# The two operands of the opening's norm move from the tag of the decay floors' logits into two tiles of their own

## The chip, the cores and the metric

The kernel runs on one core of a Trainium2 chip. The metric is the device time of one execution in microseconds (us); a program's time is the median of its runs. The core's engines each run their own list of instructions strictly in order: PE (matmul; PEld is its weight load), DVE (vector), ACT (scalar and activation), POOL, and SP, which here only issues transfers. An instruction that waits holds up everything behind it on its engine; an issue of a transfer that waits holds up all later issues of SP.

## The reference, cut to what matters

The kernel computes two layers of a decoder trunk on 512 tokens of width 1024. Only the very beginning is touched: the first normalisation and the first feed-forward block.

```python
def rms_norm(x, gain):
    inv = lax.rsqrt(jnp.mean(x * x, axis=-1, keepdims=True) + EPS)
    return (x * inv) * gain

def swiglu(h, w_in, w_out):                       # w_in 1024 x 5632, w_out 2816 x 1024
    gate, up = jnp.split(h @ w_in, 2, axis=-1)
    return (jax.nn.silu(gate) * up) @ w_out

x = x + 0.5 * swiglu(rms_norm(x, ffn1_norm[0]), ffn1_w_in[0], ffn1_w_out[0])   # the opening is in here
...                                               # three token mixers; a second swiglu; the same for layer 1
```

One of the mixers, HGRN2, has a decay with a floor per channel: `lower_bounds`, a softmax over the layers of `hgrn_lb_logits` (2 x 256 numbers, 2 KB), is computed once, in the opening, and first used much later.

## The kernel before, in words

**Products.** x is held transposed, as eight tiles of 128 features by 512 tokens. Every float32 product is made of three matmuls: each operand is parted into a high part (rounded to the format fp32r by a copy on ACT) and a low part (operand minus high part, a subtraction on DVE), and PE adds high*high, high*low and low*high. In `mm3` these are lines 318, 324 and 325; in the opening's own loop all three are line 1710.

**Weights.** A *granule* is two steps k of 128 rows of the weights by 512 columns, 512 KB. `granule` (line 282) loads it by two transfers of 256 KB issued by SP (line 290) into a staging tile `st` (two buffers), and `parted` writes its high part (line 307, ACT) and its low part (line 308, DVE) into an `hl` tile (three buffers). An `st` buffer is free again when line 308 has read it, an `hl` buffer when PE has used it. The casts of such granules are given high priority, so the scheduler sets them as early in each engine's list as it believes their data to be there.

**The opening** (`open_stream`, line 1631). Blocks f = 0, 2, 4 of the first feed-forward (two tiles of gate and two of up columns each, four PSUM banks, 96 matmuls of 512 columns) are multiplied plainly, by `cover` (line 491); from f = 6 on an arrangement with fewer products (`halved`) takes over, with matmuls of 256 columns. During f = 0, x itself arrives: SP loads x and the weights in turn, PE transposes x (line 1647), ACT and DVE make the scaled high and low parts of x (lines 391, 392) and of the weights (lines 1666, 1667), DVE copies x (line 1732), and ACT squares it (line 407) for DVE to add up in `sqacc` (line 408). The order of these loads on SP, and of most of the rest, is given by hand (`follow`); what is not given, the scheduler orders by priority and by its own estimate of the times. These three blocks use the raw x times gain, so their products don't need the norm; the norm's factor `inv` is multiplied in when their banks are cleared (lines 548, 549).

**The norm of the opening** (`norm` in `cover`, line 503). `parted_norm` (line 418) parts `sqacc` into two tiles of 128 x 512, high by ACT, low by DVE (both line 421). `end_norm` (line 427) sums both over the features with two matmuls (line 430) into one PSUM bank, here `po`, of which there is one buffer, and makes `inv` from it: three ACT instructions (line 270), then DVE lines 414, 415 and 416. Then `halves_of_x` (line 691) makes the operands of the halved blocks from x and `inv` (lines 701 to 740).

**The logits.** Right after `norm()`, `cover` calls `lower_bounds` with one scratch tile (line 523). Its transfer (line 956) is put into SP's given order, ahead of the loads of f = 2. Its arithmetic is 20 small DVE instructions (lines 958 to 997) and two small ACT ones.

**Tags.** A tile pool gives each tag a number of buffers; a tile asked for under a tag takes one of them, and its first writer waits until the last reader of that buffer's former tile is done. Tag `g1` has two buffers. Before the change the norm's high and low part are the first two tiles of `g1`, and the scratch tile of the logits is the third. Tags `r0` and `r1`, with one buffer of 4 KB per partition each, hold quarters of the hidden activations; their first writers are lines 686 and 689, behind the clearing of f = 0.

```python
def norm():
    self.end_norm(self.bank(...), fp, self.parted_norm(fp, "g1", 2))                              # 504
    ...
self.lower_bounds(logits, fp.tile([P, T], F32, tag="g1", name=self.n("lb"), bufs=2))            # 523
self.follow("s", nc.sync.dma_start(lg, logits.rearrange("l (r p) -> p l r", p=P)))              # 956
```

Of the kernel before, what the change touches and what calls it, by code (L numbers as in the profile page):

```python
# [9 lines left out]
F32R = mybir.dt.float32r  # L10
# [13 lines left out]
P = 128  # L24
T = 512
# [131 lines left out]
class Trunk:  # L157
# [257 lines left out]
        V(nc.vector.tensor_scalar(t, t, scalar1=-0.5, scalar2=1.5, op0=ALU.mult, op1=ALU.add))  # L415
        V(nc.vector.tensor_mul(out, r, t))

    def parted_norm(self, pool, tag, bufs, keep=False):
        nc = self.nc
        hi, lo = (pool.tile([P, T], F32R, tag=tag, name=self.n("sh"), bufs=bufs) for _ in range(2))  # L420
        a, b = nc.scalar.copy(hi, self.sqacc), nc.vector.tensor_sub(lo, self.sqacc, hi)
        if keep:
            self.follow("a", a)
            self.follow("v", b)
        return hi, lo
# [65 lines left out]
    def cover(self, fp, w_in, covered, begin, then):  # L491
        nc = self.nc
        x, gain, logits = begin
        for f in range(0, covered, 2):
            banks = self.next4()

            def parts(k, kk, f=f):
                r = slice(k * P, (k + kk) * P)
                return [w_in[r, f * P : (f + 2) * P], w_in[r, FF + f * P : FF + (f + 2) * P]]

            opening = f == 0

            def norm():
                self.end_norm(
                    self.bank("pt" if self.ntog % 2 == 0 else "po"), fp,
                    self.parted_norm(fp, "g1", 2),
                )
                self.xparts = self.halves_of_x(fp)

                for _ in range(2):  # L510
                    next(self.xparts)


            jobs = [(bk, slice(c, c + P)) for bk, c in zip(banks, (0, 256, 128, 384))]
            if opening:
                self.open_stream(x, gain, fp, parts, jobs)
            else:
                self.stream([(*j, None) for j in jobs], parts, self.xact, KD, queued=f == 2)
            if opening:
                nt = iter(["xh4", "xl4", "xh5", "xl5", "xh6", "xl6", "r2", "r3", "r4", "r5"])  # L520
                self.build_consts(lambda dt: fp.tile([P, T], dt, tag=next(nt), name=self.n("c")))
                norm()
                self.lower_bounds(logits, fp.tile([P, T], F32, tag="g1", name=self.n("lb"), bufs=2))
            if f == 2:
                for _ in self.xparts:
                    pass
            if f + 4 == covered or f + 2 == covered:
                next(then)
            if opening:
                self.table(SILU)  # L530

            def finish(i, f=f, banks=banks):
                self.finish(fp, f, i, banks[2 * i], banks[2 * i + 1], f + 2 == covered)

            if f + 2 < covered:
                for i in range(2):
                    finish(i)
        return finish
# [20 lines left out]
    def enter(self, fp, w_in, then):  # L559
        nc = self.nc  # L560
        H = T // 2
        A, V = (lambda i, e=e: self.follow(e, i) for e in "av")

        def stream(f, banks, given):
            def parts(k, kk):
                r = slice(k * P, (k + kk) * P)
                return [w_in[r, f * P : (f + 2) * P], w_in[r, FF + f * P : FF + (f + 2) * P]]

            return self.stream_steps(
                [(bk, slice(c, c + P), None) for bk, c in zip(banks, (0, 256, 128, 384))],  # L570
                parts, self.xact, KD, given=given,
            )

        ba = self.next4()
        first = stream(0, ba, lambda k: k == KD - 2)
        for _ in range(4):
            next(first)
        parts = self.parted_norm(fp, "g1", 2, True)
        nb = self.bank("pt" if self.ntog % 2 == 0 else "po")
        bb = self.next4()  # L580
        second = stream(2, bb, lambda k: True)
        self.ngain = self.const.tile([P, KD], F32, tag="ngain", name=self.n("ngain"))
        A(nc.scalar.activation(self.ngain, self.gain, AF.Copy, scale=-1.0))
        next(second)
        self.end_norm(nb, fp, parts, True)
        self.table(SILU)
        next(first, None)
        next(then)
        X, self.xc, lows = {}, {}, {}

        def quarter(a, b):
            X[a, b] = t = fp.tile([P, 4, H], F32, tag=f"r{2 + 2 * a + b}", name=self.n("xn"))
            for k in range(4):
                i = 4 * a + k
                V(nc.vector.scalar_tensor_tensor(
                    out=t[:, k, :], in0=self.xT[:, i, b * H : (b + 1) * H],
                    scalar=(self.gain if a == b else self.ngain)[:, i : i + 1],
                    in1=self.inv[:, b * H : (b + 1) * H], op0=ALU.mult, op1=ALU.mult,
                ))

        def high(name):
            c = ORDER_IN.index(name)
            src, other = X[SUM[name]], name in NEGATIVE
            hi, lo = (
                fp.tile([P, 4, H], F32R, tag=f"x{w}{c}", name=self.n("xc")) for w in "hl"
            )
            self.xc[name] = hi, lo
            A(nc.scalar.activation(hi, src, AF.Copy, scale=-1.0) if other else nc.scalar.copy(hi, src))

            def low():  # L610
                V(nc.vector.scalar_tensor_tensor(
                    out=lo, in0=src, scalar=-1.0, in1=hi, op0=ALU.mult, op1=ALU.subtract
                ) if other else nc.vector.tensor_sub(lo, src, hi))

            lows[name] = low

        def add(x, y):
            V(nc.vector.tensor_add(X[x], X[x], X[y]))

        def both(name):  # L620
            high(name)
            lows[name]()

        def row():
            next(second)
            next(second, None)

        cleared = {}

        def clear(f, i):  # L630
            banks = bb if f else ba
            cleared[f, i] = self.clear(fp, banks[2 * i], banks[2 * i + 1], True)

        def values(f, i):
            self.values(fp, f, i, *cleared.pop((f, i)), True)

        quarter(0, 0)
        high("P1")
        quarter(1, 0)
        lows["P1"]()  # L640
        next(second)
        next(second)
        high("P2")
        quarter(0, 1)
        lows["P2"]()
        quarter(1, 1)
        next(second)
        next(second)
        add((0, 0), (0, 1))
        high("P5")  # L650
        clear(0, 0)
        lows["P5"]()
        next(second)
        next(second)
        next(second, None)
        add((0, 0), (1, 1))
        high("P6")
        self.given["total"]()
        lows["P6"]()
        self.given["prepare"](0)  # L660
        self.given["prepare"](1)
        clear(0, 1)
        add((0, 1), (1, 1))
        next(then)
        values(0, 0)
        self.entry = {
            0: lambda: both("P7"),
            1: lambda: (both("P3"), add((0, 0), (1, 0))),
            3: lambda: both("P4"),
            7: lambda: values(0, 1),  # L670
            9: lambda: clear(2, 0),
            10: lambda: values(2, 0),
            12: lambda: clear(2, 1),
            13: lambda: values(2, 1),
        }
# [323 lines left out]
    def mix(self, l, w, w_out, conv_w, out_gain, q_gain, k_gain, f_bias, next_gain):  # L999
# [3 lines left out]
        with tc.tile_pool(name=self.n("mix"), bufs=1) as mp:  # L1003
# [47 lines left out]
            with tc.tile_pool(name=self.n("hg"), bufs=1) as hp:  # L1051
                self.tt, self.tb = "t", 3
                norm = lambda: self.end_norm(
                    self.bank("pt"), hp, self.parted_norm(hp, self.tt, self.tb)
                )
                bz = features([(H_F, 256)], ("mm", "mm"), norm)
                bg = features([(H_G, 256)], ("mm", "po"))
# [728 lines left out]
```

## Time and profile before

| | |
|---|---|
| median of 3 runs | 1832.18 us (1830.63 to 1835.08) |
| profiled execution | 1827.76 us, its span from first to last instruction 1826.0 us |
| mean granted PE clock | 0.998 |
| PE busy | 1809.0 us, 99% of the span |
| DVE busy | 1466.3 us, 80% |
| ACT busy | 989.9 us, 54% |

The profile shows one execution. In the timeline view each row gives start, duration (us), engine, line, operation and tiles, and in brackets the idle time of that engine before it and what ended it. Rows named SPq are issues of transfers. The waits view sums such idle time: total, times, longest. The windows view gives each engine's busy time in a stretch; its column PEclk is the granted clock of PE (1.00 is full speed).

### The profile page before, as it was taken

The page shows a single profiled execution, that of the slowest core. Times are in us where ns is not written, and L with a number is a line of the kernel's source. Part 1 is how long each engine was busy: PE and PEld are TensorE (multiplying, and loading weights), DVE is VectorE, ACT ScalarE, POOL GpSimd, SP SyncE. Part 2 cuts the span into 40 slices and gives each one's busy share as a digit, 9 for nine tenths or more (in the row PEclk, how much of TensorE's full clock was granted, in tenths as well). Part 3 has the DMA queues.
Part 4 walks back from the last instruction along what each step waited for, and adds up shares of the span by engine and source line. Part 5 has one row for each costly group of instructions (what it writes and reads, how often), then busy time and mean ns, then how long its engine had stood idle before and what let it go on. Part 6 is the DMA issues. An engine that isn't in the chain of part 4 may idle for free.

```text
span 1826.0 us, 34831 instructions
## 1 busy us (share of the span) xinstructions
PE 1809.0 (99%) x14345; PEld 1684.3 (92%) x14345; DVE 1466.3 (80%) x2017; ACT 989.9 (54%) x1402; POOL 169.5 (9%) x168
## 2 busy tenths in 40 slices
PE   8999999999999999999999999999999999999999
PEld 6899999899878899999889999998997788999997
DVE  8788888676797988879678887866858878888883
ACT  5455555454675565555445555555547665555551
POOL 0011020100000001112001111201000000020210
PEclk9999999999999999999999999999999999999999
DMA  5849684233322767868265787813333228677762
GB/s 147 233 109 199 171 174 113 70 88 83 87 71 92 216 141 163 191 168 174 81 193 137 162 191 194 165 64 82 83 82 82 76 93 231 162 152 195 153 137 92
DMA packets 243935, 250.94 MB, mean 137 GB/s; under 512 B 18457, under 2 KB 229153, under 8 KB 243777
## 3 DMA queue, kind: packets, MB, share of 16 engines
q1 hardware_dynamic: 189872, 182.38, 32.8%
q0 software_dynamic: 53600, 66.09, 22.7%
q8 instruction: 112, 1.84, 0.4%
q14 instruction: 47, 0.38, 0.1%
q10 hardware_dynamic: 304, 0.27, 0.0%
HBM read 223.98 MB, written 2.10 MB: 124 GB/s over the span
## 4 chain that ended last, share of the span: by engine, by line
PE 92%; DVE 3%; ACT 3%; DMA 1%; issue 1%; SPq 0%; ACTq 0%; DVEq 0%
PE mm L318 13%; PE mm L325 13%; PE mm L324 13%; PE sc L325 6%; PE sc L324 6%; PE sc L318 6%; PE pt L318 6%; PE pt L324 6%; PE pt L325 6%; PE po L318 3%; PE po L324 3%; PE po L325 3%; PE po L1543 1%; PE sc L1710 1%; PE pt L1710 1%
## 5 line engine op out<-in xcount | busy, mean ns | idle before, releaser
L786 ACT CAST hl<-w 128x1024 fp32r<-128x1024 f32 x322 | 337.5, 1051 | 317.9 <-PE mm L325 76.8
L788 DVE TENSOR_TENSOR hl<-w,hl 128x1024 fp32r<-128x1024 f32 x322 | 392.7, 1222 | 85.8 <-ACT hl L786 85.6
L307 ACT CAST hl<-st 128x512 fp32r<-128x512 f32 (+2 forms) x188 | 142.2, 756 | 190.3 <-PE po L325 67.8
L308 DVE TENSOR_TENSOR hl<-st,hl 128x512 fp32r<-128x512 f32 (+2 forms) x188 | 161.6, 860 | 100.3 <-ACT hl L307 98.6
L318 PE MATMUL mm<-xc,hl 128*128 128x256 f32 (+1 forms) x732 | 201.7, 276 | 0.5 <-ACT g L897 0.5
L325 PE MATMUL mm<-xc,hl 128*128 128x256 f32 x728 | 201.6, 277 | 0.0
L324 PE MATMUL mm<-xc,hl 128*128 128x256 f32 x728 | 201.5, 277 | 0.0
L325 PE MATMUL sc<-xc,hl 128*128 128x256 f32 x528 | 146.0, 277 | 0.0
L318 PE MATMUL sc<-xc,hl 128*128 128x256 f32 (+1 forms) x530 | 146.0, 276 | 0.0
L324 PE MATMUL sc<-xc,hl 128*128 128x256 f32 x528 | 145.9, 276 | 0.0
L318 PEld LDWEIGHTS mm<-xc,hl 128*128 128x128 f32 x732 | 137.3, 188 | 0.8 <-ACT g L897 0.7
L324 PEld LDWEIGHTS mm<-xc,hl 128*128 128x128 f32 x728 | 137.0, 188 | 0.0
L325 PEld LDWEIGHTS mm<-xc,hl 128*128 128x128 f32 x728 | 136.7, 188 | 0.1
L318 PE MATMUL pt<-xc,hl 128*128 128x256 f32 (+1 forms) x484 | 132.9, 276 | 0.0
L324 PE MATMUL pt<-xc,hl 128*128 128x256 f32 x480 | 132.7, 277 | 0.0
L325 PE MATMUL pt<-xc,hl 128*128 128x256 f32 x480 | 132.5, 276 | 0.0
L318 PE MATMUL mm<-x,hl 128*128 128x512 f32 x272 | 108.5, 399 | 6.0 <-ACT hl L307 5.6
L324 PE MATMUL mm<-x,hl 128*128 128x512 f32 x272 | 107.5, 395 | 0.0
L325 PE MATMUL mm<-x,hl 128*128 128x512 f32 x272 | 107.1, 394 | 0.0
L318 PEld LDWEIGHTS sc<-xc,hl 128*128 128x128 f32 x530 | 99.5, 188 | 0.2
L325 PEld LDWEIGHTS sc<-xc,hl 128*128 128x128 f32 x528 | 99.1, 188 | 0.1
L324 PEld LDWEIGHTS sc<-xc,hl 128*128 128x128 f32 x528 | 99.1, 188 | 0.0
(510 smaller groups left out, 5618.2 us busy)
## 6 DMA issues: line engine op xcount, KB each, us to landing
w<-in_ffn_w_in_dram SPq DMA_DIRECT2D x140, 512.0 KB, 5.2
w<-in_ffn_w_out_dram SPq DMA_DIRECT2D x64, 512.0 KB, 4.5
w<-in_ffn_w_out_dram POOLq DMA_DIRECT2D x56, 512.0 KB, 8.6
st<-in_w_mix_in_dram SPq DMA_DIRECT2D x88, 256.0 KB, 2.7
st<-in_ffn_w_in_dram SPq DMA_DIRECT2D x70, 256.0 KB, 3.3
w<-in_ffn_w_in_dram POOLq DMA_DIRECT2D x35, 512.0 KB, 8.5
w<-S POOLq DMA_DIRECT2D x35, 512.0 KB, 4.8
st<-in_ffn_w_out_dram SPq DMA_DIRECT2D x24, 512.0 KB, 4.6
```

The costliest lines, as they stand in the source:

```text
L307: a = nc.scalar.copy(hi, src[:, c : c + w])
L308: b = nc.vector.tensor_sub(lo, src[:, c : c + w], hi)
L318: i = nc.tensor.matmul(acc[:, c], ah, bh[:, c], start=first and c.start == 0, stop=False, skip_group_check=True,)
L324: nc.tensor.matmul(acc, ah, bl, start=False, stop=False, skip_group_check=True)
L325: i = nc.tensor.matmul(acc, al, bh, start=False, stop=last, skip_group_check=True)
L786: A(nc.scalar.copy(hi, src))
L788: return lambda: V(nc.vector.tensor_sub(lo, src, hi))
L1543: nc.tensor.matmul(self.ob[:, t0 + u * P : t0 + 2 * P], V[:, j, h % 4].rearrange("p a d -> p (a d)"), part[:, j, u:, :].rearrange("p i t - ...
L1710: E(nc.tensor.matmul(acc, wh[j][l][:, cols], (self.xh, self.xl)[r][k + j], start=k + j == 0 and which == 0, stop=k + j == KD - 1 and which ...
```

## The change

`parted_norm` takes one tag for each of its two tiles. In the opening these become `r0` and `r1`; the two other callers pass the tags that they had. The logits' scratch tile keeps `g1` and is now its first tile.

```diff
-    def parted_norm(self, pool, tag, bufs, keep=False):
+    def parted_norm(self, pool, tags, bufs, keep=False):
         nc = self.nc
-        hi, lo = (pool.tile([P, T], F32R, tag=tag, name=self.n("sh"), bufs=bufs) for _ in range(2))
+        hi, lo = (pool.tile([P, T], F32R, tag=tag, name=self.n("sh"), bufs=bufs) for tag in tags)
@@ cover
-                    self.parted_norm(fp, "g1", 2),
+                    self.parted_norm(fp, ("r0", "r1"), 1),
@@ enter
-        parts = self.parted_norm(fp, "g1", 2, True)
+        parts = self.parted_norm(fp, ("g1", "g1"), 2, True)
@@ mix
-                    self.bank("pt"), hp, self.parted_norm(hp, self.tt, self.tb)
+                    self.bank("pt"), hp, self.parted_norm(hp, (self.tt,) * 2, self.tb)
```

The number of instructions and of bytes moved stays the same. The scheduler's lists differ in the opening only.

## The prediction

> **What bounds the kernel now.** I read the shares on the page first, then what PE waited for, what SP's issues waited for, then the opening row by row in the timeline.
>
> ```profile
> PE 1809.0 (99%) x14345; PEld 1684.3 (92%) x14345; DVE 1466.3 (80%) x2017; ACT 989.9 (54%) x1402; POOL 169.5 (9%) x168
> ```
>
> PE bounds the whole; only time in which PE stands still or runs slowly can be won. The largest of PE's waits in the first 150 us, then the one among those of SP's issues that bears on it (total, times, longest):
>
> ```profile
> PE mm L318 <- ACT hl L307: 5.6, 1, 5.6
> ```
>
> ```profile
> SPq L956 <- DVE sh L421: 15.7, 1, 15.7
> ```
>
> PE's largest wait is for the first weights of block f = 2. SP could not load them, because the 2 KB of logits ahead of them stood 15.7 us for a `g1` buffer until the norm's low part (L421) had been made, and a little longer until PE had used it. The rows:
>
> ```profile
> 19.99 0.67 DVE L1667 TENSOR_TENSOR hl<-st,hl 128x512 fp32r<-128x512 f32 x1
> ...
> 24.50 0.69 ACT L391 ACTIVATE x<-po,gain 128x512 fp32r<-128x512 f32 x1
> 25.08 0.62 ACT L1666 CAST hl<-st 128x512 fp32r<-128x512 f32 x1
> ...
> 26.02 0.75 DVE L392 SCALAR_TENSOR_TENSOR x<-po,gain,x 128x512 fp32r<-128x512 f32 x1
> 26.38 2.93 PE L1710 MATMUL sc<-x,hl 128*128 128x512 f32 x12
> 26.68 0.68 DVE L1667 TENSOR_TENSOR hl<-st,hl 128x512 fp32r<-128x512 f32 x1
> 27.28 0.69 DVE L1732 COPY xT<-mm 128x512 f32<-128x512 f32 x1
> ...
> 29.14 2.89 PE L1710 MATMUL pt<-x,hl 128*128 128x512 f32 x12
> ...
> 30.22 0.62 ACT L421 CAST sh<-sqa 128x512 fp32r<-128x512 f32 x1 [0.96 <-DVE sqa L408]
> 30.87 0.69 DVE L421 TENSOR_TENSOR sh<-sqa,sh 128x512 fp32r<-128x512 f32 x1 [0.32 <-ACT sh L421]
> ...
> 31.87 0.63 PE L430 MATMUL po<-sh,ones_mean 128*128 128x512 f32 x2
> 32.30 0.37 SPq L956 DMA_DIRECT2D lb<-in_hgrn_lb_logits_dram  x1
> ...
> 34.64 0.69 DVE L414 SCALAR_TENSOR_TENSOR nt<-po,nt 128x512 f32<-128x512 f32 x1 [3.08 <-ACT nt L270]
> 35.25 0.16 DVE L958 COPY lb<-lb 128x2 f32<-128x2 f32 x1
> ...
> 36.98 1.05 ACT L307 CAST hl<-st 128x1024 fp32r<-128x1024 f32 x1 [2.38 <-DMA st<-in_ffn_w_in_dram]
> 37.94 0.20 ACT L270 ACTIVATE lb<-lb 128x4 f32<-128x4 f32 x1
> 38.06 1.23 DVE L308 TENSOR_TENSOR hl<-st,hl 128x1024 fp32r<-128x1024 f32 x1 [0.21 <-ACT hl L307]
> 38.08 0.80 PE L318 MATMUL mm<-x,hl 128*128 128x512 f32 x1 [5.58 <-ACT hl L307]
> ```
>
> The staging buffer for f = 2 is free at 20.66 (the first row's end), but the issues begin only behind the logits' (32.30) and the first cast at 36.98. To count the loss, two fixed points on PE and the clock:
>
> ```profile
> 44.30 0.39 PE L325 MATMUL mm<-x,hl 128*128 128x512 f32 x1
> ```
>
> ```profile
> 83.28 0.33 PE L318 MATMUL mm<-xc,hl 128*128 128x128 f32 x2
> ```
>
> ```profile
> 34.00:35.00 1.00, 0.00 (x0) 0.00 (x0) 0.36 (x1) 0.61 (x1) 0.00 (x0) 0.77 0.99 242
> ...
> 41.00:42.00 1.00, 1.00 (x5) 0.77 (x4) 1.00 (x4) 0.00 (x0) 0.00 (x0) 0.82 1.03 356
> ```
>
> 44.30 is the 21st matmul of f = 2, and 83.28 the first halved product, 172 matmuls later: (83.28 - 44.30)/172 = 0.227 us each, without a gap. From 26.38 to 44.30 PE starts 24 matmuls of f = 0, 2 of the norm and 20 of f = 2: 46 x 0.227 = 10.44 of 17.92 us. **7.48 us are lost**: 5.8 of standing, and 1.7 because the clock (PEclk, the third figure from the right) is halved: 0.77 in 34 to 35 puts the drop at about 34.5, 2.0 us after PE stopped, and 0.82 in 41 to 42 the return at about 41.4. That is the most that can be won.
>
> **The change, part by part.** (1) With the norm's operands in `r0` and `r1`, the logits need no buffer of theirs. Nothing is waited for there: the next writers of these tags are behind `inv`. The issue follows k = 6's weights at about 16, and f = 2's first granule, A, is issued when its `st` buffer is free, at 20.7 and 21.1. Landings after a pair's second issue, from the transfer view: a pair alone; the pair issued at 32.78 with another behind it; the pair at 46.15, behind 2.5 MB:
>
> ```profile
> DMA to landing us min/median/max: 2.9/2.9/2.9
> ```
>
> ```profile
> DMA to landing us min/median/max: 3.6/3.6/3.6
> ```
>
> ```profile
> DMA to landing us min/median/max: 7.6/7.6/7.6
> ```
>
> A is alone: landed at 24.0.
>
> (2) The lists that the built program holds for each engine change with it. On ACT (k = 7's two casts of f = 0 are x_48 and the second hl_299; 507, 537 and 567 are granules A, B and C of f = 2):
>
> ```
> L307 hl_507 / L391 x_48 / L1666 hl_299 / L407 / L407 / L307 hl_537 / L421 sh / L270 lb / L307 hl_567 / L270 nr
> ```
>
> DVE likewise does the copy of x and A's low part ahead of k = 7's, B's ahead of the norm's, C's and the logits' arithmetic ahead of L414. PE gets five matmuls of f = 2 within the last 24 of f = 0, and two between the norm's two.
>
> (3) ACT: A's cast starts at 24.50 and takes 1.05, the next one overlapping its last 0.1 (as 25.08 does that of 24.50), so k = 7's casts end at 26.65. DVE: the copy at 26.02, A's low part 26.62 to 27.85 (1.23, overlapped by 0.1), then k = 7's, ending at 28.51 and 29.10, 1.74 later than now. PE: k = 7's first matmul fits at 27.06; A's first two follow; the third waits for 27.85 (0.16); the next, of k = 7, for 28.51 (0.44); the rest runs through. f = 0 is done at 33.54 with five matmuls of f = 2 inside. **Waits 0.60.**
>
> (4) B takes A's staging buffer in the new program (before: k = 6's), so it is issued at 27.9 and 28.33. C follows at 29.1, so between alone (2.9) and followed at once (3.6) I take 3.2: landed at 31.5. On ACT the norm's high part now stands *behind* B's cast: 31.6 to 32.6, then 32.5 to 33.15, where it was 30.22. DVE: B's low part to 33.8, the norm's 33.8 to 34.5. PE's first norm matmul is in time at 33.54, two of f = 2 follow, the second would fit at 34.22 and goes at 34.53. **Wait 0.31.** Had B landed after 3.6, 0.75.
>
> (5) From the norm's second matmul (31.87 + 0.23) to L414 it takes 2.54 now: L414 at 37.07, done at 37.76. DVE gets through C's low part and 12 small instructions of the logits (0.16, row 35.25; 0.2 where one waits for the one before) by then: 34.4 + 1.1 + 12 x 0.13 on the mean = 37.1. The `po` bank of the norm is f = 2's fourth: the 21st matmul waits for L414. Thirteen others stand between and fill PE to 37.71. **Wait 0.1; the 21st starts at 37.8 instead of 44.30.** No gap reaches 2 us, so the half clock goes too.
>
> (6) Is the lead kept up to 83.28, which becomes 77.0? Rows for that: DVE's work, its last piece that the first halved product needs, and the second granule of f = 4, whose cast waited for its transfer:
>
> ```profile
> 26.02:77.96 51.94, 46.36 (x198) 37.64 (x197) 45.80 (x87) 23.88 (x29) 1.44 (x1) 0.93 0.66 193
> ```
>
> ```profile
> 58.03 1.05 ACT L307 CAST hl<-st 128x1024 fp32r<-128x1024 f32 x1 [2.68 <-DMA st<-in_ffn_w_in_dram]
> ...
> 76.74 1.22 DVE L788 TENSOR_TENSOR hl<-w,hl 128x1024 fp32r<-128x1024 f32 x1
> ```
>
> DVE ends its part at 77.96, 5.3 us before PE needs it, with 6.1 idle. The same 45.8 us and 0.8 that are moved ahead of it end at 72.6 plus the idle time left (0.4 for B, up to 1.2 for that granule): about 74, so it still covers, with less to spare. That granule's staging buffer comes free with the low part of f = 2's fourth granule, by the same walk 5.4 us earlier than now; its own low part stands ahead of the clearing of f = 0's banks (L548). If it lands by 50, as it may since all loads before it start 7 us earlier, nothing waits. If it lands only 5.4 us earlier than now, at 52.6, its low part is done at 54.9 and the last bank is free at 58.1, where PE wants it at 57.1. I take 0.2 of 0 to 1.0, nearer to nothing because the whole queue moves. From 77 on PE waits for the same things relative to itself as now.
>
> **Sum**: lost 0.60 + 0.31 + 0.1 + 0.2 = 1.2 instead of 7.48: **6.3 us won**. The profiled execution becomes 1827.76 - 6.3 = 1821.5 and the median, 4.4 above it, 1832.18 - 6.3 = **1825.9**, 0.34% less.
>
> A rule against the row: the clock was halved 2.0 us after PE stopped. The Trainium skill, TensorE: Matmul & The Clock Gate, "What's actually happening", has the clock halved after at least one idle window of about 3.4 us; a gap of 2 to 3.4 us would then cost no clock. In the sum above neither is reached. In the next case it would save 1.7 us for landings between 5.5 and 6.9.
>
> **Rivals.** *The norm waits behind a late granule B* (a new wait for the one removed). Each us of landing past 3.2 is a us of PE at the norm. At 7.6, 4.7 us of waits, 4 of them in one gap, so again 1.7 of half clock: 0.2 won, 1832.0. For it: ACT is strictly in order. Against it: only two pairs are in flight then, and the 7.6 stood behind 2.5 MB. Between 3.6 and 7.6: 1826.3 to 1832.0.
>
> *The lead is partly given back at f = 4*: the 1.0 above, 1826.7, more if the small logits instructions, now back to back, cost DVE more than that.
>
> *Slower*: A's cast now stands ahead of k = 7's on ACT, which PE needs for f = 0. About 1.5 us of lateness are free (landing at 25.5); each further us costs one, and past a gap of 2 us the half clock's 1.7. From a landing 9 us after issue on the change loses; at 12, 1835. Nothing in flight then speaks for that.
>
> *The change does nothing*: another wait holds the issues at 32. In the built program the logits' issue waits for an early load of x only, and A for the buffer freed at 20.66. 1832.2.
>
> **How the numbers follow.** About 0.3%, 5.5 us, is what a measurement of this kernel can tell from no change; the forecast lies just beyond. Forecast 0.60 (0.8 us from the bound, and the three runs spread 4: 0.52 faster, 0.08 within), late B 0.18 (0.03 faster, 0.14 within, 0.01 slower), given back 0.12 (0.03, 0.09), nothing 0.05 (within), slower 0.05 (0.03 slower, 0.02 within). Faster 0.58, within 0.38, slower 0.04. The range: 7.5 won and 1 of spread below, 1.7 won above: 1823.5 to 1830.5.
>
> **What would show it.** Right: SP's wait at L956 gone; A's cast at 24.5; PE's 21st matmul of f = 2 near 37.8 and the first halved product near 77.0; PEclk 1.00 from 30 to 45; ACT idle before B's cast for its transfer by about 0.6. Wrong: a wait over 1 us at L430 or at the fourth bank of f = 2; a wait at f = 4's first matmuls; a halved clock anywhere there.

## The result, and the profile after

The changed kernel takes 1822.84 us (median of 6 runs, 1821.34 to 1827.41), the kernel before in the same comparison 1831.39 us (6 runs, 1829.33 to 1835.08). The ratio is 0.9957 with a 95% interval of 0.9941 to 0.9972: 8.5 us won by the medians, 5.1 to 10.8 by the interval. Two more comparisons of the same two kernels, among the experiments below, gave 7.2 and 5.2 us. The forecast was 1825.9 us, from 6.3 us won.

The profiled execution after took 1825.62 us, its span 1823.8 us, only 2.2 us less than the span before. So the span isn't the place to look; the opening is. First SP's issues in the timeline (start, duration, issue; x8 counts issues that follow each other in the view):

```profile
15.87 0.47 SPq L956 DMA_DIRECT2D lb<-in_hgrn_lb_logits_dram  x1
...
20.67 14.04 SPq L290 DMA_DIRECT2D st<-in_ffn_w_in_dram  x8
```

The logits' load goes out at 15.87 instead of 32.30, and f = 2's weights from 20.67 on. Then ACT, DVE and PE in the timeline, in the order of the prediction's steps:

```profile
24.42 1.05 ACT L307 CAST hl<-st 128x1024 fp32r<-128x1024 f32 x1 [0.16 <-DMA st<-in_ffn_w_in_dram]
...
27.87 0.50 PE L325 MATMUL mm<-x,hl 128*128 128x512 f32 x1 [0.28 <-DVE hl L308]
...
28.53 0.50 PE L1710 MATMUL sc<-x,hl 128*128 128x512 f32 x1 [0.16 <-DVE x L392]
...
31.49 1.05 ACT L307 CAST hl<-st 128x1024 fp32r<-128x1024 f32 x1 [0.52 <-DMA st<-in_ffn_w_in_dram]
...
33.70 0.40 PE L430 MATMUL po<-sh,ones_mean 128*128 128x512 f32 x1
33.72 0.69 DVE L421 TENSOR_TENSOR sh<-sqa,sh 128x512 fp32r<-128x512 f32 x1
...
34.46 0.50 PE L430 MATMUL po<-sh,ones_mean 128*128 128x512 f32 x1
...
37.21 0.69 DVE L414 SCALAR_TENSOR_TENSOR nt<-po,nt 128x512 f32<-128x512 f32 x1
...
37.96 0.50 PE L318 MATMUL po<-x,hl 128*128 128x512 f32 x1
```

```profile
77.12 0.33 PE L318 MATMUL mm<-xc,hl 128*128 128x128 f32 x2
```

The gap of 5.58 us is gone; in its place stand waits of tenths. The last row of the first of these two fences is the 21st matmul of f = 2 (37.96 instead of 44.30), the row of the other the first halved product: 77.12 instead of 83.28, a lead of 6.16 us. In the windows view PEclk, the third figure from the right, is full where it was 0.77 and 0.82:

```profile
34.00:35.00 1.00, 1.00 (x5) 0.60 (x4) 0.90 (x6) 0.78 (x1) 0.00 (x0) 1.00 0.04 11
...
41.00:42.00 1.00, 1.00 (x7) 0.81 (x6) 1.00 (x4) 1.00 (x2) 0.61 (x1) 1.00 1.05 359
```

PE does the same 14345 matmuls in both kernels, so the n-th of one can be set beside the n-th of the other. The lead by this count is 6.50 at the 160th, 6.16 from the 180th (47.7 us) to 80 us, and 6.12 still at 385 us. There 0.5 goes in a wait for DVE. After that the lead lies between 0.29 and 5.6, moves in both directions, and ends at 2.2. The largest part, 4.3 us between 1000 and 1120 us, goes without any wait of PE. The last section shows what that is: it isn't the change's.

### The profile page after: what moved, and what is told of

Read it like the earlier page. It is cut to its first block, busy times and chain, and to the rows that moved or that the text cites. A ratio compares the mean times of both kernels' runs of the same rounds, so it can differ in the third digit from the quotient of the medians.

```text
span 1823.8 us, 34831 instructions
## 1 busy us (share of the span) xinstructions
PE 1811.8 (99%) x14345; PEld 1687.0 (92%) x14345; DVE 1466.9 (80%) x2017; ACT 988.4 (54%) x1402; POOL 169.3 (9%) x168
## 4 chain that ended last, share of the span: by engine, by line
PE 90%; DVE 5%; ACT 3%; issue 1%; DMA 1%; SPq 0%; ACTq 0%; DVEq 0%
PE mm L318 13%; PE mm L325 13%; PE mm L324 13%; PE sc L325 6%; PE sc L324 6%; PE sc L318 6%; PE pt L324 6%; PE pt L318 6%; PE pt L325 6%; PE po L318 4%; PE po L324 3%; PE po L325 3%; PE po L1543 1%; DMA st<-in_w_mix_in_dram 1%; DVE hl L308 1%
```

## The experiments

In all of them the lead is 83.28 us less the start of the first halved product. The 83.28 is the first profiled execution of the kernel before; its second one has 83.88, so against that each lead is 0.60 larger. The table sets it beside the whole executions; the sections tell of each.

| kernel | first halved product, us | lead, us | median less than before's, us | ratio, 95% interval |
|---|---|---|---|---|
| changed | 77.12 | 6.16 | 8.5 | 0.9957 (0.9941 to 0.9972) |
| changed, second time | 77.68 | 5.60 | 7.2 | 0.9963 (0.9949 to 0.9976) |
| changed, third time | 77.01 | 6.27 | 5.2 | 0.9972 (0.9953 to 0.9990) |
| unchained | 77.19 | 6.09 | 8.9 | 0.9952 (0.9936 to 0.9968) |
| pool_early | 77.42 | 5.86 | 7.5 | 0.9960 (0.9948 to 0.9973) |
| one_moved | 79.31 | 3.97 | 3.8 | 0.9978 (0.9969 to 0.9987) |
| keep_clock24 | 82.00 | 1.28 | 2.2 | 0.9987 (0.9973 to 1.0001) |
| keep_clock | 84.08 | -0.80 | 0.9 | 1.0001 (0.9984 to 1.0017) |
| logits_by_pool | 84.34 | -1.06 | -0.4 | 0.9999 (0.9990 to 1.0008) |
| longer_wait | 89.48 | -6.20 | -7.7 | 1.0046 (1.0028 to 1.0063) |
| before, second time | 83.88 | -0.60 | 0.5 | 1.0001 (0.9986 to 1.0017) |

Theory: the time was lost because one load, waiting for a buffer, held SP's queue ahead of f = 2's weights. Rivals: the tags or the logits' earlier arithmetic win it; the free queue alone is enough, whatever stands where; more is won behind the opening.

### The logits by POOL, tags as before

```diff
 # kernel before
-        self.follow("s", nc.sync.dma_start(lg, logits.rearrange("l (r p) -> p l r", p=P)))
+        nc.gpsimd.dma_start(lg, logits.rearrange("l (r p) -> p l r", p=P))
```

> The kernel before with one line changed: the 2 KB of logits are asked for from POOL's queue instead of SP's; the norm's operands keep both g1 buffers, so the load still waits for the norm and the logits' arithmetic stays late. Theory (only the queue behind the waiting load cost time): SP's wait at L956 is gone from its queue, granule A's cast at 24.4 as in the changed kernel, the first halved product at 77.1 +- 0.5 instead of 83.28 (lead 6.2), and the median 6 us below before. POOL waits with the load to about 34.4, its next issue (L762) is at 41.4 in the changed kernel, so nothing comes late. Rival (the gain comes from the logits' arithmetic being done earlier, ahead of the norm's end, or from the tags themselves): the first halved product stays near 83, nothing won.

Nothing was won. The timeline of this kernel:

```profile
24.45 1.05 ACT L307 CAST hl<-st 128x1024 fp32r<-128x1024 f32 x1
...
35.37 0.92 POOL L956 DMA_DIRECT2D lb<-in_hgrn_lb_logits_dram  x1 [33.71 <-PE po L430]
...
42.32 0.48 DVE L958 COPY lb<-lb 128x2 f32<-128x2 f32 x1 [5.96 <-DMA lb<-in_hgrn_lb_logits_dram]
...
42.40 0.68 DVE L414 SCALAR_TENSOR_TENSOR nt<-po,nt 128x512 f32<-128x512 f32 x1
...
43.13 0.79 PE L318 MATMUL po<-x,hl 128*128 128x512 f32 x1 [4.88 <-DVE nt L414]
```

A's cast is as early as in the changed kernel, and the lead at PE's 160th matmul was 6.2 us: the first half of the theory holds. Then it was lost in one place. The planner had put the logits' first copy (L958) ahead of the norm's L414 on DVE. The load landed at 42.2, DVE stood for it, L414 came 5.2 us late, and PE stood for the `po` bank that L414 empties. With the half clock that followed (40.82 to 47.64 us, see the last section), 7.3 us were lost there. The expectation had this copy late but didn't ask what was queued behind it. That is a second condition: the logits have to be there when DVE comes to L958. Two runs take the two conditions apart.

### The logits by POOL, tags as changed

```diff
 # changed kernel
-        self.follow("s", nc.sync.dma_start(lg, logits.rearrange("l (r p) -> p l r", p=P)))
+        nc.gpsimd.dma_start(lg, logits.rearrange("l (r p) -> p l r", p=P))
```

> The changed kernel with the logits asked for by POOL, as in logits_by_pool, but here into a buffer that nothing is waited for, so POOL asks in the first 10 us and they lie ready long before DVE's L958. All other engines' lists are those of the changed kernel. Theory (time is won when two things hold: SP's queue is free at 20.7, and the logits are there when DVE comes to L958, which stands ahead of the norm's L414; logits_by_pool met the first and missed the second): as the changed kernel, first halved product at 77.1 to 77.7, lead 5.6 to 6.2. Rival (POOL's transfers are slow or in the weights' way by themselves, and that is what took the gain of logits_by_pool): a wait at PE's fourth bank of f = 2 again, lead below 4.

```profile
1.61 0.92 POOL L956 DMA_DIRECT2D lb<-in_hgrn_lb_logits_dram  x1
...
77.42 0.33 PE L318 MATMUL mm<-xc,hl 128*128 128x128 f32 x2
```

The load goes out at 1.61, and the lead is back, 5.86 us. So POOL as such is not what took the gain, only a load that is late.

### Tags as before, the given order of the load taken away

```diff
 # kernel before
-        self.follow("s", nc.sync.dma_start(lg, logits.rearrange("l (r p) -> p l r", p=P)))
+        nc.sync.dma_start(lg, logits.rearrange("l (r p) -> p l r", p=P))
```

> The kernel before, its tags unchanged, with the one given order taken away that put the logits' load ahead of f = 2's weights in SP's queue; the planner now puts it behind f = 2's first seven issues. The lists of PE, DVE and ACT are those of logits_by_pool. Theory (the two conditions): A's cast at 24.4, lead 6.2 at the 13th f = 2 product. The load goes when the norm's low part is made, at about 34.7; how long it takes decides: under 3.0 us, as from its issue at 32.30 to its first reader at 35.25 in before, and PE's fourth bank is free at about 38.4 instead of 37.96, lead 5.6 at the first halved product (77.7); as long as in logits_by_pool (6.8 us) and PE stands some 4 us, the clock is halved again, and the lead is about -0.5. I take 5.6. Rival (the tags or the early logits' arithmetic matter by themselves, and the queue doesn't): 0 already at the 13th f = 2 product.

```profile
34.68 0.37 SPq L956 DMA_DIRECT2D lb<-in_hgrn_lb_logits_dram  x1
...
37.25 0.17 DVE L958 COPY lb<-lb 128x2 f32<-128x2 f32 x1 [0.84 <-DMA lb<-in_hgrn_lb_logits_dram]
...
37.33 0.69 DVE L414 SCALAR_TENSOR_TENSOR nt<-po,nt 128x512 f32<-128x512 f32 x1
...
38.07 0.50 PE L318 MATMUL po<-x,hl 128*128 128x512 f32 x1
...
77.19 0.34 PE L318 MATMUL mm<-xc,hl 128*128 128x128 f32 x2
```

This is the plainest form of the theory. No tag is changed, the logits' load still goes only when the norm's low part is made (34.68), and their arithmetic is late. The edit frees the load's place in SP's queue and nothing else; the planner's lists change with it, and PE's is that of logits_by_pool. The lead is 6.09 us, no different from the change's, and so is the time. DVE stood 0.84 us at L958, which moved L414 by 0.1. The rival of the tags and of the early arithmetic falls.

### Only the high part moved

```diff
 # changed kernel
-                    self.parted_norm(fp, ("r0", "r1"), 1),
+                    self.parted_norm(fp, ("r0", "g1"), (1, 2)),
...
-        hi, lo = (pool.tile([P, T], F32R, tag=tag, name=self.n("sh"), bufs=bufs) for tag in tags)
+        hi, lo = (pool.tile([P, T], F32R, tag=tag, name=self.n("sh"), bufs=n) for tag, n in zip(tags, bufs if isinstance(bufs, tuple) else (bufs,) * 2))
```

> The changed kernel, but only the norm's high part is in an idle tile; its low part stands in one g1 buffer, the logits take the other, which nothing is waited for either. SP is as free as in the changed kernel, so granule A lands at 24 too, but the planner puts A's cast behind the norm's Ln and two Exps on ACT, and all f = 2 matmuls behind the norm's two. Theory (what counts is when A's cast is reached on ACT, the free queue only allows it): the cast at about 34.7 (nt's 33.98 + 0.63 of the kernel before), PE's first f = 2 matmul at 35.9 instead of 38.08, a gap of 3.4 us, so that the clock is halved as well: lead 2.2 if as much of f = 2 runs at the half clock as before (3.3 us), 1.1 if it comes back at 41.4 as before, 2.8 if it comes back one 3.4 us step earlier. Rival (the free queue alone wins the time): lead 6.2. Rival (the logits' arithmetic or buffers): also 6.2, as both are as in the changed kernel.

```profile
34.00 0.63 ACT L270 ACTIVATE nt<-nr 128x512 f32<-128x512 f32 x1
...
34.53 1.98 ACT L307 CAST hl<-st 128x1024 fp32r<-128x1024 f32 x2
...
35.61 0.50 PE L318 MATMUL mm<-x,hl 128*128 128x512 f32 x1 [3.09 <-ACT hl L307]
```

SP is as free as in the changed kernel (A's weights are asked for at 20.68), but the planner has set their cast behind the norm's three instructions on ACT: 34.53, and PE stands 3.09 us. That falsifies "the free queue alone wins 6.2". The lead is 3.97, though, not 2.2 as expected, because the clock stayed at 1.00: with 2.5 us less standing than before and 1.7 less of half clock, 4.2 were to be expected. The windows' rows stand in the section on the hardware.

### The wait made longer

```diff
 # kernel before
-                self.lower_bounds(logits, fp.tile([P, T], F32, tag="g1", name=self.n("lb"), bufs=2))
+                self.lower_bounds(logits, fp.tile([P, T], F32, tag="g2", name=self.n("lb"), bufs=2))
```

> The kernel before with the logits' scratch in tag g2 instead of g1: the load, first in SP's queue, waits until inv is made (L416, done at 36.5 in before) instead of 32.3, 4.2 us longer; nothing else changes but the places of some small instructions. Theory (each us by which the load holds SP's queue past the point where f = 2's weights are wanted is a us of PE): granule A's cast at 41.2 instead of 36.98, PE's gap 9.8 instead of 5.6, first halved product at 87.5 instead of 83.28, median 4 us above before (3.5 to 4.5, as the half clock may cost 1.2 instead of 1.7). Rival (what is late in before is ACT and DVE with the norm, and the queue would have had time): 0 to 1 us slower.

```profile
36.56 0.37 SPq L956 DMA_DIRECT2D lb<-in_hgrn_lb_logits_dram  x1
...
41.47 1.04 ACT L307 CAST hl<-st 128x1024 fp32r<-128x1024 f32 x1 [0.60 <-DMA st<-in_ffn_w_in_dram]
...
42.56 0.80 PE L318 MATMUL mm<-x,hl 128*128 128x512 f32 x1 [10.09 <-ACT hl L307]
```

```profile
70.20 0.69 DVE L548 TENSOR_TENSOR gi<-pt,inv 128x512 f32<-128x512 f32 x1
...
70.95 0.50 PE L318 MATMUL pt<-x,hl 128*128 128x512 f32 x1 [1.34 <-DVE gi L548]
```

Issued 4.26 us later than before, the load costs 4.53 us at PE's 160th matmul: us for us, as the theory has it. The expectation missed 1.7 us more, and the median is 7.7 us above before's, not 3.5 to 4.5. At f = 4 (second fence) PE waits for DVE to clear a bank. The edit moved more than the small instructions that the expectation names: the planner set this clearing, which ran at 52.98 us in before, behind the last of the logits' arithmetic, at 70.20. The clearing of a `pt` bank at f = 4 cost the changed kernel 0 to 0.5 us.

### The clock alone

```diff
 # kernel before, behind norm()
+                z = fp.tile([P, T], F32, tag="u2", name=self.n("z"), bufs=2)[:, :P]
+                nc.vector.memset(z, 0.0)
+                spare = self.bank("mm")
+                for _ in range(36):
+                    self.follow("p", nc.tensor.matmul(spare[:, :P], z, z, start=True, stop=True))
```

> The kernel before with 36 products of a tile of zeros into a spare bank behind the norm's two; PE does them in the gap, 32.5 to about 36.4 (0.107 us each, as the four transposes of L1647 in 0.43), and then stands 1.7 us until f = 2's first weights. The work itself is as in before; the outputs too. Theory (the loss of 7.5 us in before is 5.6 of standing and 1.7 of half clock, apart from each other): f = 2's first product at 38.1 as in before, PEclk 1.00 throughout 34 to 42, first halved product at 81.6 instead of 83.28, lead 1.7. Rival (products of zeros don't hold the clock, or the clock was not what made those matmuls slow): lead 0.

```profile
32.49 8.20 PE L527 MATMUL mm<-z 128*128 128x128 f32 x72
...
40.44 0.48 PE L318 MATMUL mm<-x,hl 128*128 128x512 f32 x1
```

The 36 products are 72 matmuls in the trace and took 8.0 us, so they delayed f = 2 by 2.4 us themselves. The lead is -0.80, and the run settles nothing by its lead. With 24 of them:

> As keep_clock, with 24 products of zeros instead of 36: there each took 0.22 us, not 0.107 (8.0 us for 36, so that PE reached f = 2 at 40.44, 2.4 us late). 24 take 5.3 us, 32.5 to 37.85, and f = 2's weights are cast at 38.1 as in before. Theory (standing and half clock are separate terms, 5.6 and 1.7): PEclk 1.00 throughout 34 to 42, f = 2's first product at 38.1, the first halved product at 81.6, lead 1.7; the 5.6 us of the gap stay lost. Rival (the clock is not what made those matmuls slow): lead 0.

```profile
32.27 5.52 PE L527 MATMUL mm<-z 128*128 128x128 f32 x48
...
38.20 0.50 PE L318 MATMUL mm<-x,hl 128*128 128x512 f32 x1 [0.41 <-ACT hl L307]
...
43.02 0.39 PE L325 MATMUL mm<-x,hl 128*128 128x512 f32 x1
```

From the first to the 21st matmul of f = 2 it takes 43.02 - 38.20 = 4.82 us instead of 44.30 - 38.08 = 6.22. PEclk is 1.00 throughout. That is 1.4 us for the clock, and 0.26 more went into a wait for A's low part that the half clock had hidden: together the 1.7 of the prediction. The lead is 1.28 and not 1.7 because of that wait and because f = 2 starts 0.12 later than in before. Standing and clock are separate terms.

### Repeats

> The changed kernel once more, for a narrower interval and a second trace. Theory (the time lay in the held SP queue alone, and PE's lead of 6.2 us at the first halved product is all there is to win): won by the medians 6.2 us with the runs' spread, 5 to 7.5, ratio 0.9966; PE's first halved product at 77.1 again. Rival (a second gain that the one profile doesn't show, since the medians so far differ by 8.5): 8 to 9 us won again, ratio 0.9955 or lower. For the scatter after 400 us: if the stretches in which all matmuls run some 4% slower belong to the program, they stand at 1020 to 1120 us again; if they are chance, they stand elsewhere and the span differs by a few us from 1823.8.

> The kernel before against itself, for the scatter and a second trace of it. All four versions whose lead at the first halved product is 5.6 to 6.2 us were 7.2 to 8.9 us faster by their medians. If that surplus is scatter, this comparison gives 0 with an interval some 2 us wide to each side, and now and then a stretch of about 100 us in its trace in which PE starts 257 instead of 267 matmuls in 30 us at a granted clock of 1.00, as in four of the seven versions' traces and not in the first trace of before. If there is something in before that the first trace doesn't show, a stretch without such a slow pace but with a wait that the changed kernel's traces lack.

> The changed kernel a third time, on the same chip as before_again. Theory (the lead in the opening is all): 5.6 to 6.2 us won by the medians within the interval, and a mean of the three comparisons within 1.5 us of 6. Rival (about 2 us more are won behind the opening): 7.5 to 9 again, mean of the three near 8, and the lead over before_again grows behind 80 us apart from stretches of slow pace.

The three comparisons of the two kernels give 8.5, 7.2 and 5.2 us by the medians, 7.0 on the mean, and the kernel before against itself 0.5 with an interval from 0.9986 to 1.0017, some 2.9 us to each side. Each interval of the three holds the traces' lead of 5.6 to 6.3. Behind the opening, one wait stands in both executions of before and in none of the three of the changed kernel (this row is of before):

```profile
1448.20 0.30 PE L1521 MATMUL sc<-KA,QA 128*128 128x128 f32 x1 [0.41 <-DMA KA<-KA]
```

By the distances of PE's starts it is worth 0.67 us. The three versions unchained, pool_early and logits_by_pool lack it too, the other four have it; why wasn't tested. Against it, at 385 us the three executions of the changed kernel lose 0.2 to 0.7 us more than those of before. The rival of a second gain of about 2 us isn't borne out; that a us or two more is won somewhere isn't excluded either.

## Why the prediction was right, point by point

- **(1) The issue at 16, A issued at 20.7, landed at 24.0**: the issues are right. A landed 3.3 us after its second issue, at 24.4, not 2.9, so ACT idled 0.16 for it and the cast began at 24.42 (forecast 24.50). SP's wait at L956 is gone.
- **(3) A's cast ahead of k = 7's costs 0.60**: PE's two waits end at 27.87 and 28.53, where the step put them (27.85 and 28.51). Their cost, by the distance of the starts from 0.23, is 0.45 + 0.43 = 0.88; the brackets of the rows, 0.28 and 0.16, give idle time alone. It is more than 0.60 because PE came there 0.34 earlier than in the first trace of before (26.04 instead of 26.38), as it did in before's second execution too. The step's own times give 0.54: its first wait, from 27.74 to 27.85, is 0.11. PE's first norm matmul started at 33.70 instead of 33.54. The rival built on it (a landing so late that it loses) wasn't tried on the chip.
- **(4) B landed at 31.5, PE waits 0.31 at the norm**: B's cast at 31.49 after 0.52 idle, the norm's low part at 33.72. PE's second norm matmul started at 34.46 (forecast 34.53) and lost 0.07 behind the f = 2 matmul at 34.16 (0.23 each), since PE itself was 0.16 later; when B came 0.2 later in the second execution it started at 34.66. The late B of the first rival didn't occur.
- **(5) L414 at 37.07, the 21st matmul at 37.8, wait 0.1**: 37.21, 37.96, 0.15 by the distance from 37.58 + 0.23. Right, but too narrowly told: step (2) had seen that the logits' arithmetic stands ahead of L414, and step (5) priced it as busy time only. In logits_by_pool it became a wait of 5 us. In the changed kernel the load is issued at 15.87 and read at 30.32.
- **(6) The lead kept but for 0.2 of 0 to 1.0**: 0 in the changed kernel's first and third trace, 0.46 in its second, 0.19 in pool_early, 0 in unchained. The granule's cast began at 51.44 and 52.32 in the first two, each time as its transfer landed: between the step's two cases (50 and 52.6). The row of the second execution, with PE's weight load waiting for DVE's clearing, is the one that the step named:

```profile
57.83 0.19 PEld L318 LDWEIGHTS pt<-x,hl 128*128 128x128 f32 x1 [0.48 <-DVE ui L549]
```

- **The sum**: 6.3 us; the lead is 6.16, 5.60 and 6.27 in three executions against the first trace of before, 0.60 more against its second. What the forecast had right are the times at which the waits end, to 0.2. Its single terms are up to 0.3 off, in both directions, because a wait ends when ACT or DVE is done, whenever PE comes to it.
- **The half clock**: its 1.7 us are right for the execution that was profiled (1.6 by the clock's own times, see the last section), but the rule used, that a gap of 2 us brings it, is wrong. one_moved stood 3.09 us without it, and before_again lost 2.3 us to it from the same gap. The forecast didn't hang on this, since its gaps are all under 0.5; the price of the rival with a late B did.
- **The time**: 1822.84 instead of 1825.9, 0.7 below the range. The kernel before was 0.8 lower in this comparison, and the medians showed 2.2 more than the 6.3. Later comparisons showed 0.9 more and 1.1 less, and the first one's interval (5.1 to 10.8 us) holds 6.3. So the miss fits the scatter of a median of six; the range had allowed 1 us of spread on that side.

## What to carry to other kernels

A load's cost isn't its bytes: 2 KB that wait for a buffer hold all that is queued behind them, here for 16 us. Look at the first wait of the issuing queue, and ask whether the load can have an idle buffer or a later place in the queue; both gave the same 6 us. Then follow each reader of that load in its own in-order queue: freeing one queue moved the same delay to DVE when the data came late, and the gain was gone.

## What the runs showed of the hardware

**The clock goes by windows of 3.41 us that run by themselves.** From the windows view, one fence for each kernel, the slices in which the clock fell and came back. First longer_wait:

```profile
35.00:36.00 1.00, 0.00 (x0) 0.00 (x0) 0.93 (x3) 0.00 (x0) 0.00 (x0) 0.87 0.00 0
...
45.00:46.00 1.00, 1.00 (x4) 0.81 (x3) 1.00 (x2) 0.00 (x0) 0.00 (x0) 0.51 0.79 237
```

logits_by_pool:

```profile
40.00:41.00 1.00, 0.00 (x0) 0.00 (x0) 0.00 (x0) 0.00 (x0) 0.00 (x0) 0.91 0.93 260
...
47.00:48.00 1.00, 1.00 (x4) 0.76 (x4) 0.83 (x1) 1.00 (x2) 0.00 (x0) 0.68 1.13 181
```

The second execution of before:

```profile
38.10 0.80 PE L318 MATMUL mm<-x,hl 128*128 128x512 f32 x1 [5.64 <-ACT hl L307]
```

```profile
35.00:36.00 1.00, 0.00 (x0) 0.00 (x0) 1.00 (x5) 0.00 (x0) 0.00 (x0) 0.91 1.01 286
...
42.00:43.00 1.00, 1.00 (x4) 0.75 (x4) 1.00 (x4) 0.16 (x1) 0.00 (x0) 0.68 0.78 164
```

A slice with 0.87 was at full clock for 0.74 of it and at half for the rest. So the clock fell at 35.74, 40.82 and 35.82 and was back at 45.98, 47.64 and 42.64: 10.24, 6.82 and 6.82 us, 3, 2 and 2 times 3.41. In the first trace of before it is 34.54 to 41.36, 6.82 again. From PE's stop to the fall it took 3.3, 2.6, 3.4 and 2.0 us, and one_moved's 3.09 us went by without one:

```profile
34.00:35.00 1.00, 0.00 (x0) 0.00 (x0) 0.90 (x7) 1.00 (x2) 0.00 (x0) 1.00 0.00 0
35.00:36.00 1.00, 0.39 (x2) 0.35 (x3) 1.00 (x5) 1.00 (x2) 0.00 (x0) 1.00 0.00 0
```

That fits windows whose ends lie anywhere relative to the program: at a window's end the clock is halved if PE was mostly idle in it, and restored if it was mostly busy. Going back 3.41 us from each fall and return, windows with 40% and less of PE work were followed by the half clock, such with 96% and more by the full clock. The traces' clock records show that the windows run on from the start: their first entry, full clock, stands at 7.23 us in before, 5.10 in its second execution, 6.68 in logits_by_pool and 5.03 in longer_wait, and the falls come 27.31, 30.72, 34.13 and 30.72 us later, 8, 9, 10 and 9 times 3.413. In one_moved the first entry is at 6.96, so windows ended at 34.27 and 37.68. PE worked 49% of the one (until 32.52) and 61% of the other (from 35.61), and the clock stayed: the share below which it falls lies between 40 and 49% here. The Trainium skill, TensorE: Matmul & The Clock Gate, "What's actually happening", gives a free-running window of 3413 ns, and the traces agree with that length. It has the fall come after an idle window; here the window before the fall was 40% busy in the first trace of before (31.13 to 34.54, PE at work until 32.50). So the same gap of 5.6 us cost 1.6 us in one execution of before ((41.36 - 38.08)/2) and 2.3 in the other ((42.64 - 38.10)/2).

**This small load took longer through POOL than through SP.** In logits_by_pool and pool_early the 2 KB took 6.8 and 5.1 us from issue to landing, the latter before anything waited for it; through SP, in unchained, the first reader started 2.57 us after the issue. Which part of the 6.8 is POOL's and which the weights' that moved beside it isn't settled.

**All matmuls can be 4% slower for some 110 us at full granted clock.** From the windows view of PE alone (PE busy and matmuls, PEclk, DMA share, GB/s), the same 30 us in the first and the second execution of before:

```profile
720.00:750.00 30.00, 30.00 (x267) 1.00 0.98 185
```

```profile
720.00:750.00 30.00, 30.00 (x257) 1.00 0.87 163
```

and in the changed kernel's first and second execution:

```profile
1040.00:1070.00 30.00, 30.00 (x257) 1.00 0.88 163
```

```profile
1040.00:1070.00 30.00, 30.00 (x267) 1.00 0.92 178
```

PE is full in each, without a wait. Of all twelve executions, compared by their n-th matmuls, seven had one or two such stretches of some 110 us, 4.4 us each: from about 680, 1002 or 1580 us on. Versions had them in one execution and not in another. They explain why spans differ by several us when the opening differs by none, and why a lead has to be read where it is made. What brings them on stays open.
